# Storing the recurrence's normaliser vectors as rows transposed on chip

## The chip, the cores and the metric

The kernel runs on one core of a Trainium2 chip. Its time is the device time of one execution in microseconds (us); the kernel before has a median of 781.07 us over three runs (779.24 to 781.85). One further execution was profiled, and every row below is from it: it took 777.49 us, of which the span from the first to the last instruction is 775.7 us.

## The reference

One step of a layer with three head groups over a shared input projection: differential attention (A), a matrix-memory recurrence (B, mLSTM) and cross-attention into a memory (M), for a prompt of 1024 tokens and, beside it, for 8 decoding streams of 16 tokens with a cache of 1024. Group B is what matters here. For each of its 4 heads of dimension 64 it carries a matrix C and a vector n, the normaliser, from chunk to chunk:

```python
C = decay[..., None, None] * C0 + jnp.einsum('bhs,bhsd,bhse->bhde', wS, k, v)
n = decay[..., None] * n0 + jnp.einsum('bhs,bhsd->bhd', wS, k)
```

The final states are outputs of the kernel: `p_C` (4 heads x 64 x 64) and `p_n` (4 x 64) for the prompt, `s_C` (8 streams x 4 x 64 x 64) and `s_n` (8 x 4 x 64) for the decoding streams. All are 4-byte floats in device memory.

## The kernel before, in words

Nine row tiles of 128 tokens are worked on: tiles 0 to 7 are the prompt, tile 8 (`DEC`) holds the 8 x 16 decoding tokens. Phases follow each other (A0 to A3, G, M, B0, B1, O0, O1): each loads and splits a block of weights and projects all nine tiles through it (three passes of high and low parts, `project`, matmuls of L97 into the PSUM banks `ps_z` and `ps_y`). What is done with a projected tile is a generator in stages, and a pipe advances those of earlier tiles while later tiles are projected (`feed`). Attention of the decoding streams (`dec_attention`, with key and value loads `kc`, `vc` of 512 KB each) is woven in through phases M, B0 and B1.

Phases B0 and B1 (`pr` 0 and 1) do two heads each. `b_stages` is the work on one tile: `mlstm_in` (L1012) copies and transposes q and k, `mlstm_scores` (L1038) loads rows of `mtd` broadcast over the partitions into `mb` (L1042) and makes the decay mask from them on POOL (L1043) and ACT (L1045), then come the products and the new state. For the prompt the state of a pair of heads is one tile `csn` of 128 x 130: partition (head, d), columns 0 to 63 of a head's 65 being C and the 65th being n. After the last prompt tile (L1149) four stores are issued for the pair, C and n of each head. For the decoding streams (`mlstm_decode`, L1077) the state is the tile `C0`, 128 partitions (head, d) by 8 streams by 65 columns. It has one buffer (`bufs=1`): the load for pair 1 (L1079) can be issued only when everything that reads pair 0's tile is done, the two stores at L1111 and L1112 among it. In B0 the decoding tile goes first, in B1 third.

In both cases n is spread over the partitions, one 4-byte element (per stream) in each, and it is stored from there: 1024 elements for one pair's `s_n` (L1112), 64 for one head's `p_n` (L1152).

All loads and stores are issued by SyncE (SP) from one in-order list. The order of the instructions of every engine is worked out by a scheduler from its own model of durations, with the priorities that the code sets (`ahead`); within an engine that order is then fixed, and an instruction that waits holds up all behind it. PSUM tiles with the tag `tp`, into which all transposes write, have two buffers.

Of the kernel before, what the change touches and what calls it, by code (L numbers as in the profile page):

```python
# [11 lines left out]
F32 = mybir.dt.float32  # L12
# [8 lines left out]
P = 128  # L21
# [3 lines left out]
NPT = 8  # L25
# [35 lines left out]
def hymba_step(ctx: ExitStack, tc: tile.TileContext, a: dict, o: dict):  # L61
    nc = tc.nc
    V, S, G, PE, SY = nc.vector, nc.scalar, nc.gpsimd, nc.tensor, nc.sync

    def pool(name, side="left"):
        return tc.tile_pool(name=name, bufs=1, side=side, reuse_waits="tile")
# [5 lines left out]
    def bank(tag):  # L72
        bufs = {"z": 2, "y": 1, "tp": 2, "s": 2, "av": 1}[tag]
        return ps.tile([P, 512], F32, tag=tag, name=f"ps_{tag}", bufs=bufs)
# [3 lines left out]
    def copy(e, out, in_):  # L78
        if e == "S":
            S.copy(out, in_)  # L80
        else:
            ENG[e].tensor_copy(out, in_)
# [13 lines left out]
    def mm(out, lhsT, rhs, start=True, stop=True):  # L96
        PE.matmul(out, lhsT, rhs, start=start, stop=stop)  # L97
# [11 lines left out]
    def bc(ap, n):  # L109

        return ap.unsqueeze(len(ap.shape)).broadcast_to(list(ap.shape) + [n])

    def rep(ap, n):

        return ap.unsqueeze(1).broadcast_to([ap.shape[0], n] + list(ap.shape[1:]))

    def heads(ap, h):
        return ap.rearrange("p (h e) -> p h e", h=h)

    def flat(ap):  # L120
        return ap.rearrange("p a b -> p (a b)")


    ident = cpool.tile([P, P], F32, name="ident")
# [887 lines left out]
    def mlstm_in(bw, nb, bufs, t, pr, z):  # L1012

        hs = slice(2 * pr, 2 * pr + 2)
        vx, qn, cs = bufs
        qp, qn = qn, bw.tile([P, 2, 64], F32, tag="bqn", name="bqn", bufs=nb)
        S.copy(flat(qn), z[:, 0:128])
        kg = bw.tile([P, 2, 64], F32, tag="kg", name="kg", bufs=nb)
        S.activation(flat(kg), z[:, 128:256], AF.Copy, scale=0.125)
        kw = bw.tile([P, 2, 64], F32, tag="kw", name="kw", bufs=nb)  # L1020
        G.tensor_tensor(kw, kg, bc(wsN[:, t, hs], 64), ALU.mult)
        S.copy(vx[:, :, 0:64], heads(z[:, 256:384], 2))
        gt = bw.tile([P, P], F32, tag="bgt", name="bgt", bufs=nb)
        SY.dma_start(out=gt, in_=gated[t][:, 512 + pr * P:512 + (pr + 1) * P])
        th = bw.tile([P, P], F32, tag="bth", name="bth", bufs=2)
        S.activation(th, z[:, 384:512], AF.Tanh, scale=0.5)
        V.scalar_tensor_tensor(gt, th, 1.0, gt, ALU.add, ALU.mult)
        tp = bank("tp").rearrange("p (a b) -> p a b", a=4)
        PE.transpose(tp[:, 0], flat(kg), ident)
        PE.transpose(tp[:, 1], flat(qn), ident)  # L1030
        qk = bw.tile([P, 2, P], F32, tag="qk", name="qk", bufs=nb)
        V.tensor_copy(qk, tp[:, 0:2])
        for i in range(2):
            sl = slice(i * 64, i * 64 + 64)
            copy("VS"[i], qp[sl, i * P:(i + 1) * P], tp[sl, 1])
        return qk, kw, gt

    def mlstm_scores(bw, nb, t, pr, mask, qk, qp):  # L1038

        mb = bw.tile([P, 2, P], F32, tag="mb", name="mb", bufs=nb)  # L1040
        r0 = t * 4 + 2 * pr
        SY.dma_start(out=flat(mb), in_=mtd[r0:r0 + 2, :].rearrange("h t -> (h t)").partition_broadcast(P))  # L1042
        G.tensor_tensor(mb, rep(mask, 2), mb, ALU.subtract)  # L1043
        for h2 in range(2):
            S.activation(mb[:, h2], mb[:, h2], AF.Exp, bias=aN[:, t, 2 * pr + h2:2 * pr + h2 + 1])  # L1045
        st = bank("s")[:, 0:256]
        mm(st, qk[:, 0], qp)
        V.tensor_tensor(flat(mb), st, flat(mb), ALU.mult)
        return mb

    def mlstm_out(bw, nb, t, pr, nm, carried, dst, gate):
# [22 lines left out]
            )  # L1074
        SY.dma_start(out=dst, in_=flat(hb))

    def mlstm_decode(pr, z, bufs):  # L1077
        C0 = bw.tile([P, 8, 65], F32, tag="C0", name="C0", bufs=1)
        SY.dma_start(out=C0, in_=a["Cn"][pr])  # L1079
        qk, kw, gt = mlstm_in(bw, nb, bufs, DEC, pr, z)  # L1080
        yield
        at = mlstm_scores(bw, nb, DEC, pr, maskd, qk, bufs[1])
        yield
        vx = bufs[0]
        for i in range(2):
            V.tensor_copy(
                gqz.rearrange("p (c i) x -> p c i x", i=2)[:, :, i, i * 16:i * 16 + 16],
                qk[:, 1].rearrange("p (c i q) -> p c i q", i=2, q=16)[:, :, i],
            )
        nmf = bank("s")  # L1090
        nm, carried = heads(nmf[:, 0:130], 2), heads(nmf[:, 130:260], 2)
        for i in range(2):
            for h2 in range(2):
                sl = slice(h2 * 64, h2 * 64 + 64)
                copy("VG"[h2], csd[sl, :, h2 * 65:h2 * 65 + 65], C0[sl, i::2])
            for c in range(4):
                mm(nmf[c * 32:c * 32 + 32, 130:260], gqz[:, 2 * c + i, :], csd[:, c, :], i == 0, i == 1)
        for h2 in range(2):
            mm(nm[:, h2], at[:, h2], vx[:, h2])
        mlstm_out(bw, nb, DEC, pr, nm, carried, mixd[DEC][:, 512 + pr * P:640 + pr * P], gt)  # L1100
        V.tensor_tensor(C0, C0, bc(dec[:, DEC, pr], 65), ALU.mult)
        for c in range(0, NB, 4):
            km = bw.tile([P, 4, P], F32, tag="km", name="km", bufs=2)
            (G, V)[c // 4].tensor_tensor(km, rep(flat(kw), 4), bc(bm[:, c:c + 4], P), ALU.mult)
            up = heads(bank("s")[:, 0:260], 4)
            for j in range(4):
                for h2 in range(2):
                    mm(up[h2 * 64:h2 * 64 + 64, j], km[:, j, h2 * 64:h2 * 64 + 64], vx[:, h2])
            V.tensor_tensor(C0[:, c:c + 4], up, C0[:, c:c + 4], ALU.add)
        hs = slice(2 * pr, 2 * pr + 2)  # L1110
        SY.dma_start(out=o["s_C"][0, :, hs].rearrange("b h d e -> (h d) b e"), in_=C0[:, :, 0:64])  # L1111
        SY.dma_start(  # L1112
            out=o["s_n"][0, :, hs].rearrange("b h (d o) -> (h d) b o", o=1), in_=C0[:, :, 64:65]
        )

    cst = {}

    def b_stages(pr, t, i_):
        def run(z):
            if t == DEC:  # L1120
                yield from mlstm_decode(pr, z, bufs2[i_ % nb])
                return
            bufs = bufs2[i_ % nb]
            vx, qn, csn = bufs
            qk, kw, gt = mlstm_in(bw, nb, bufs, t, pr, z)
            yield
            at = mlstm_scores(bw, nb, t, pr, maskp, qk, qn)
            yield
            nmf = bank("s")
            nm, carried = heads(nmf[:, 0:130], 2), None  # L1130
            cs = cst.get(pr)
            if t:
                carried = heads(nmf[:, 130:260], 2)
                mm(flat(carried), qk[:, 1], cs)
            for h2 in range(2):
                mm(nm[:, h2], at[:, h2], vx[:, h2])


            up = nmf[:, 260:390]
            mm(up, flat(kw), flat(vx))  # L1140
            for h2 in range(2):
                sl, cc = slice(h2 * 64, h2 * 64 + 64), slice(h2 * 65, h2 * 65 + 65)
                if t == 0:
                    V.tensor_copy(csn[sl, cc], up[sl, cc])
                else:
                    V.scalar_tensor_tensor(
                        csn[sl, cc], cs[sl, cc], dec[sl, t, pr, 0:1], up[sl, cc], ALU.mult, ALU.add
                    )
                if t == NPT - 1:  # L1149
                    h = 2 * pr + h2  # L1150
                    SY.dma_start(out=o["p_C"][0, 0, h], in_=csn[sl, h2 * 65:h2 * 65 + 64])
                    SY.dma_start(  # L1152
                        out=o["p_n"][0, 0, h].rearrange("(d o) -> d o", o=1),
                        in_=csn[sl, h2 * 65 + 64:h2 * 65 + 65],
                    )
            cst[pr] = csn
            mlstm_out(bw, nb, t, pr, nm, carried, mixd[t][:, 512 + pr * P:512 + (pr + 1) * P], gt)

        return run
# [65 lines left out]
    bw = ctx.enter_context(pool("bwork", "right"))  # L1225
# [121 lines left out]
```

## Time and profile before

| what | value |
|---|---|
| median of three runs | 781.07 us (779.24 to 781.85) |
| the profiled execution, and its span | 777.49 us, 775.7 us |
| busy: TensorE (PE), VectorE (DVE), ScalarE (ACT), GpSimd (POOL) | 730.5, 471.8, 333.3, 237.1 us |
| mean granted TensorE clock | 0.982 of full speed |
| DMA queues, share of 16 engines over the span | 43.1% |
| chain that ended last: PE, DVE, DMA | 77%, 8%, 7% |

PE is the matmul row and PEld its weight loads. A granted clock of 1.00 is TensorE's upper level (2.4 GHz), 0.50 the lower (1.2 GHz). Times of events are microseconds from the span's start. In a timeline row, the bracket at the end tells how long the engine had been idle and whose end it waited for. The name `C` in the trace is the tile `C0`, `cs` the tile `csn`.

### The profile page before, as it was taken

To read this page: it belongs to the slowest core of one execution; us is meant where nothing else is said; L and a number is where in the kernel's file an instruction comes from. 1 tells how busy PE (TensorE), PEld (TensorE's weight loads), DVE (VectorE), ACT (ScalarE), POOL (GpSimd) and SP (SyncE) were. 2 spreads that over 40 slices of the span, in tenths; PEclk is the share of its full clock that TensorE was granted. 3 is DMA by queue.
4 is the path that set the end of the run, shared out by engine and by line. 5 is a ranking of instruction groups with operands and counts; after the bars stand their busy time and mean duration, and the time that the engine had idled before them with its cause. 6 is when DMAs were issued, how large, how long until landed. Compare 5 with 4: busy or idle time off the path is not lost.

```text
span 775.7 us, 14506 instructions
## 1 busy us (share of the span) xinstructions
PE 730.5 (94%) x4944; PEld 603.6 (78%) x4944; DVE 471.8 (61%) x1460; ACT 333.3 (43%) x978; POOL 237.1 (31%) x336
## 2 busy tenths in 40 slices
PE   7998899999999999999999899699999948999998
PEld 6776688878888888998878677467777737778887
DVE  6888786677788778678685844136833535842011
ACT  6666635574564466465354452224422323411200
POOL 6653451232133222336311413102211215521500
PEclk9999999999999999999999999889999979999999
DMA  8733430151014112415401529358978316984332
GB/s 314 278 110 94 148 99 28 34 160 49 19 51 124 49 28 63 120 55 144 152 15 18 188 73 336 95 183 301 327 222 248 120 41 222 310 208 136 109 108 95
DMA packets 84388, 106.20 MB, mean 137 GB/s; under 512 B 16054, under 2 KB 52698, under 8 KB 84314
## 3 DMA queue, kind: packets, MB, share of 16 engines
q1 hardware_dynamic: 84314, 105.28, 43.1%
q8 instruction: 39, 0.64, 0.4%
q14 instruction: 35, 0.29, 0.1%
HBM read 86.01 MB, written 19.23 MB: 136 GB/s over the span
## 4 chain that ended last, share of the span: by engine, by line
PE 77%; DVE 8%; DMA 7%; issue 3%; POOL 2%; ACT 2%; SPq 0%; DVEq 0%; POOLq 0%; ACTq 0%
PE ps_z L97 40%; PE ps_y L97 16%; PE ps_s L97 8%; PE ps_av L97 6%; DMA mb<-mtd 3%; DMA wraw<-in_w_in_dram 2%; PE ps_tp L461 2%; DMA out_dram<-C 1%; DVE wl L240 1%; PE ps_tp L202 1%; PE ps_tp L406 1%; PE ps_tp L902 1%; DVE xT L296 1%; POOL asm L135 1%; DMA mxt<-in_mem_prompt_dram 1%
## 5 line engine op out<-in xcount | busy, mean ns | idle before, releaser
L97 PE MATMUL ps_z<-wh,htl 128*128 128x512 f32 (+2 forms) x552 | 212.7, 387 | 0.0
L97 PE MATMUL ps_z<-wh,hth 128*128 128x512 f32 (+2 forms) x552 | 199.2, 393 | 3.9 <-ACT hth L282 2.6
L97 PE MATMUL ps_z<-wl,hth 128*128 128x512 f32 (+2 forms) x552 | 184.1, 387 | 0.0
L97 PEld LDWEIGHTS ps_z<-wh,hth 128*128 128x128 f32 x552 | 103.0, 189 | 25.2 <-ACT hth L282 2.8
L97 PEld LDWEIGHTS ps_z<-wh,htl 128*128 128x128 f32 x552 | 104.2, 189 | 18.2 <-DVE htl L283 0.4
L97 PEld LDWEIGHTS ps_z<-wl,hth 128*128 128x128 f32 x552 | 103.1, 189 | 18.5 <-issue 0.8
L97 PE MATMUL ps_y<-wh,htl 128*128 128x512 f32 (+2 forms) x176 | 66.5, 380 | 0.0
L97 PE MATMUL ps_y<-wh,hth 128*128 128x512 f32 (+2 forms) x176 | 64.3, 386 | 0.0
L135 POOL TENSOR_TENSOR asm<-asm,nhalf 128x4 f32<-128x4 f32 x36 | 39.6, 1100 | 75.0 <-DVE asm L139 59.7
L445 ACT ACTIVATE usx<-usx,usm 128x1024 f32<-128x1024 f32 (+7 forms) x64 | 49.7, 778 | 29.1 <-DVE usm L439 26.8
L97 PE MATMUL ps_y<-wl,hth 128*128 128x512 f32 (+2 forms) x176 | 60.4, 376 | 0.1
L240 DVE SCALAR_TENSOR_TENSOR wl<-wraw,gnm,wh 128x512 fp32r<-128x512 f32 (+1 forms) x62 | 47.3, 785 | 4.2 <-ACT wh L233 4.0
L233 ACT ACTIVATE wh<-wraw,gnm 128x512 fp32r<-128x512 f32 (+1 forms) x56 | 38.1, 707 | 20.6 <-DMA wraw<-in_w_in_dram 18.5
L97 PE MATMUL ps_s<-aqk 128*128 128x256 f32 (+1 forms) x160 | 42.0, 288 | 2.2 <-ACT aqk L414 2.2
L439 DVE CUSTOM_DVE_ANT_0 usx<-ps_s,tab 128x512 f32<-128x512 f32 (+3 forms) x64 | 37.0, 587 | 9.0 <-PE ps_s L97 7.6
L135 POOL TENSOR_TENSOR usm<-usm,nhalf 128x1 f32<-128x1 f32 x32 | 19.6, 612 | 72.9 <-DVE usm L469 68.4
L97 PE MATMUL ps_s<-akl,aqk 128*128 128x256 f32 (+1 forms) x160 | 41.0, 283 | 0.0
L97 PE MATMUL ps_av<-avg,wth 128*128 128x128 f32 x288 | 38.7, 276 | 0.2 <-DVE uot L471 0.2
L97 PEld LDWEIGHTS ps_av<-avg,wth 128*128 128x128 f32 x288 | 36.9, 191 | 2.5 <-ACT wth L462 0.6
L97 PEld LDWEIGHTS ps_y<-wh,hth 128*128 128x128 f32 x176 | 33.8, 193 | 5.7
L97 PEld LDWEIGHTS ps_y<-wh,htl 128*128 128x128 f32 x176 | 33.9, 193 | 5.3
L97 PEld LDWEIGHTS ps_y<-wl,hth 128*128 128x128 f32 x176 | 33.0, 188 | 5.7 <-DVE wl L240 0.5
(448 smaller groups left out, 1379.6 us busy)
## 6 DMA issues: line engine op xcount, KB each, us to landing
kc<-in_kT_dram SPq DMA_DIRECT2D x32, 512.0 KB, 6.5
vc<-in_cache_attn_v_dram SPq DMA_DIRECT2D x32, 512.0 KB, 7.0
wraw<-in_w_in_dram SPq DMA_DIRECT2D x56, 256.0 KB, 3.1
omx<-mixd SPq DMA_DIRECT2D x9, 512.0 KB, 6.4
out_dram<-oxt SPq DMA_DIRECT2D x17, 256.0 KB, 2.1
xt<-in_x_prompt_dram SPq DMA_DIRECT2D x8, 512.0 KB, 7.5
wraw<-in_w_out_dram SPq DMA_DIRECT2D x16, 256.0 KB, 4.1
oxt<-in_x_prompt_dram SPq DMA_DIRECT2D x16, 256.0 KB, 3.6
```

Of the source, the lines that this page charges most:

```text
L97: PE.matmul(out, lhsT, rhs, start=start, stop=stop)
L135: G.tensor_tensor(dst, ss, nhalf[:, 0:ss.shape[1]], ALU.pow)
L202: PE.transpose(tv[:, i, :], src[:, (c + i) * P:(c + i + 1) * P], ident)
L233: S.activation(wh[:, 0:n], raw[:, 0:n], AF.Copy, scale=g_)
L240: V.scalar_tensor_tensor(wl[:, 0:n], raw[:, 0:n], g_, f(wh[:, 0:n]), ALU.mult, ALU.subtract)
L296: V.scalar_tensor_tensor(xT[:, cs], xT[:, cs], math.sqrt(D), rep(rb, 4), ALU.mult, ALU.mult)
L406: PE.transpose(tp[:, i], flat(nd[:, 2 * i:2 * i + 2]), ident)
L439: V.tensor_tensor_reduce(s_[:, c * 512:c * 512 + w], sp[:, 0:w], tab[:, tx:tx + w], -slope, BIG if c == 0 else sm[:, m:m + 1], ALU.add, AL ...
L445: S.activation(s_[:, 0:nk], s_[:, 0:nk], AF.Exp, bias=last, scale=-1.0, accum_out=sm[:, 4 + m:5 + m])
L461: PE.transpose(tp[:, i], sx[0][:, (c + i) * P:(c + i + 1) * P], ident)
L902: PE.transpose(tp[0:pn, c - c0, :], se[:, c * P:c * P + pn], ident)
```

## The change

A helper `store_n` takes the columns that hold n, transposes them on TensorE into a PSUM tile (n rows of 128), copies that to an SBUF tile `nt` on ScalarE, and stores rows. For `s_n` the store at L1112 becomes one store of 8 rows of 128 elements (512 bytes each, both heads of a pair for one stream). For `p_n` the two stores of a pair at L1152 become two stores of one row of 64 elements each (256 bytes), taken from the diagonal blocks of a 2 x 128 tile, issued after both heads are updated. The stores of C stay as they are.

```diff
+    def store_n(dst, cols, diag=False):
+
+        n = cols.shape[1]
+        tp = bank("tp")
+        PE.transpose(tp[0:n, 0:P], cols, ident)
+        nt = bw.tile([8, P], F32, tag="nt", name="nt", bufs=1)
+        S.copy(nt[0:n], tp[0:n, 0:P])
+        if diag:
+            for h2 in range(2):
+                SY.dma_start(out=dst[h2:h2 + 1], in_=nt[h2:h2 + 1, h2 * 64:h2 * 64 + 64])
+        else:
+            SY.dma_start(out=dst, in_=nt[0:n])
+
     def mlstm_decode(pr, z, bufs):
...
         SY.dma_start(out=o["s_C"][0, :, hs].rearrange("b h d e -> (h d) b e"), in_=C0[:, :, 0:64])
-        SY.dma_start(
-            out=o["s_n"][0, :, hs].rearrange("b h (d o) -> (h d) b o", o=1), in_=C0[:, :, 64:65]
-        )
+        store_n(o["s_n"][0, :, hs].rearrange("b h d -> b (h d)"), C0[:, :, 64])
...
                     SY.dma_start(out=o["p_C"][0, 0, h], in_=csn[sl, h2 * 65:h2 * 65 + 64])
-                    SY.dma_start(
-                        out=o["p_n"][0, 0, h].rearrange("(d o) -> d o", o=1),
-                        in_=csn[sl, h2 * 65 + 64:h2 * 65 + 65],
-                    )
+            if t == NPT - 1:
+                hs = slice(2 * pr, 2 * pr + 2)
+                store_n(o["p_n"][0, 0, hs], csn[:, 64::65], True)
```

## Rows read from the trace of the kernel before

**Rows 1.** The page's busy times: engine, busy us, share, instructions.
```profile
PE 730.5 (94%) x4944; PEld 603.6 (78%) x4944; DVE 471.8 (61%) x1460; ACT 333.3 (43%) x978; POOL 237.1 (31%) x336
```

**Rows 2.** Chain that ended last, 484 to 512 us: start, us, what.
```profile
485.87 11.63 DMA out_dram<-C
497.56 3.33 DMA C<-in_Cn_dram
...
500.92 0.29 DVE csd L82
...
504.45 0.29 DVE ewt L82
...
505.44 1.96 PE ps_av L97 x16
...
508.01 3.15 PE ps_z L97 x9
```

**Rows 3.** Timeline of PE, 494 to 506 us: start, us, instruction, idle before.
```profile
494.88 1.96 PE L97 MATMUL ps_y<-vc,ewt 128*32 128x128 f32 x64
504.78 0.66 PE L97 MATMUL ps_y<-vn,ewt 128*32 128x128 f32 x8 [7.94 <-DVE ewt L82]
```

**Rows 4.** Windows: stretch, length, PE PEld DVE ACT POOL busy, PEclk, DMA, GB/s.
```profile
490.00:492.00 2.00, 2.00 (x13) 1.56 (x12) 0.07 (x1) 0.40 (x1) 0.00 (x0) 1.00 0.00 0
...
500.00:502.00 2.00, 0.00 (x0) 0.00 (x0) 0.65 (x3) 0.30 (x2) 0.46 (x1) 0.50 0.71 188
...
626.00:628.00 2.00, 0.00 (x0) 0.00 (x0) 0.00 (x0) 0.00 (x0) 0.00 (x0) 1.00 0.05 4
...
630.00:632.00 2.00, 0.00 (x0) 0.00 (x0) 0.00 (x0) 0.00 (x0) 0.00 (x0) 0.50 0.01 3
```

**Rows 5.** Timeline of SP, 484 to 488 us.
```profile
485.43 0.39 SPq L1111 DMA_DIRECT2D out_dram<-C  x1
```

**Rows 6.** Line L1111 by itself: issue to landing of the store of C.
```profile
DMA to landing us min/median/max: 2.7/2.9/3.1
```

**Rows 7.** Chain that ended last, 600 to 650 us.
```profile
621.70 13.30 DMA mb<-mtd
...
636.78 1.22 PE ps_y L97 x4
638.00 1.20 PE ps_s L97 x2
639.20 7.45 PE ps_y L97 x24
```

**Rows 8.** Timeline of PE, 624 to 640 us.
```profile
636.78 1.22 PE L97 MATMUL ps_y<-ems,sr 128*128 128x128 f32 x4 [10.97 <-ACT ems L914]
```

**Rows 9.** Tile mb: issue to landing of its 18 loads.
```profile
DMA to landing us min/median/max: 3.0/5.0/13.3
```

**Rows 10.** Chain that ended last, 560 to 600 us.
```profile
565.93 2.28 PE ps_z L97 x9
...
576.08 6.77 DMA mb<-mtd
...
588.33 1.02 PE ps_av L97 x16
...
590.22 0.45 PE ps_y L97 x4
590.66 0.43 PE ps_s L97 x2
...
591.70 5.46 PE ps_y L97 x24
```

**Rows 11.** Timeline of PE, 584 to 592 us.
```profile
585.58 0.28 PE L902 MATMUL ps_tp<-ident,se 128*16 128x128 f32 x1 [1.25 <-DVE ewt L82]
```

**Rows 12.** Timeline of ACT, 588 to 590 us.
```profile
589.07 0.26 ACT L80 COPY qn<-ps_tp 64x128 f32<-64x128 f32 x1 [0.78 <-DVE qn L82]
```

**Rows 13.** Waits: who waited for whom, us in total, times, longest.
```profile
ACT mb L1045 <- POOL mb L1043: 43.6, 13, 11.4
```

## The prediction

> **What bounds the kernel now.** I read the page first: PE is busy for 94% of the span [rows 1], so a stall elsewhere counts only where it opens a hole in PE. Then I read the chain of waits in order of time and looked for pieces that are no PE work. Most are short. The long ones in the last 300 us are three DMA pieces, and each lies beside one of the stores of n. For each I took the PE timeline (is PE idle, and who ends it?) and the windows (what do the DMA engines do meanwhile?).
>
> Hole 1, pair 0's decoding state. The store of C is issued at 485.43 [rows 5], that of n at 485.87; the chain then waits 11.63 us for a store out of C0, reloads C0 for 3.33 us, and DVE's copy `csd`, which needs it, starts at 500.92 [rows 2]. DVE is in order, and the small copy `ewt` queued behind it starts at 504.45 [rows 2]. PE had ended its work at 494.88 + 1.96 = 496.84 and idles 7.94 us for that copy [rows 3]. During the wait the DMA engines show a share of 0.00 and 0 GB/s [rows 4]: nothing else is being moved. The clock is at its lower level in 500:502, after PE had stopped [rows 4].
>
> Hole 2, pair 1's decoding state. A load of `mb` issued at 621.70, just behind that pair's stores, takes 13.30 us [rows 7], where the median load of `mb` takes 5.0 and the fastest 3.0 [rows 9]. PE idles 10.97 us, from 625.81 to 636.78 [rows 8]; the DMA share is 0.05 and 0.01 in that time and the clock falls again [rows 4].
>
> Hole 3, pair 0's prompt state. A load of `mb` at 576.08, with the four stores of C and n issued right after it, takes 6.77 us [rows 10], and PE idles 1.25 us [rows 11]. Pair 1's prompt stores have no such wait in the chain: PE has projections queued there, and I cost that end at nothing.
>
> **The change, part by part.** What goes is 2 x 1024 + 4 x 64 = 2304 stored elements of 4 bytes; what comes is 2 stores of 8 rows and 4 of one row. The number of issues on SP stays the same, six.
>
> Hole 1: the reload of C0 now waits for the store of C and for a transpose that reads C0. The store of C lands 2.7 to 3.1 us after its issue [rows 6], with 2.9 at 488.3. The reload takes its 3.33 to 491.7, some 9.2 us before 500.92, and the copy `ewt`, 3.53 + 0.29 behind `csd` [rows 2], ends at about 495.5. That is before PE is through at 496.84, so the whole 7.94 goes. What is late next is PE itself; 1.3 us of slack is left. Next is the clock: 16 `ps_av` matmuls took 1.96 at the lower level against 1.02 later, 9 of `ps_z` took 3.15 against 2.28 [rows 2, 10]; 0.94 + 0.87 = 1.81 returns if PE doesn't stop. Together 9.75.
>
> Hole 2: with `mb` landing L after 621.70, PE can go on at 621.70 + L + 1.78, where 1.78 is the way from landing (635.00) to PE (636.78) today [rows 7, 8]. L = 3.0 gives 626.48, L = 5.0 gives 628.48; the hole shrinks to 0.67 or 2.67. I take the median, so 10.97 - 2.67 = 8.30. The clock term: 4 `ps_y` 1.22 against 0.45, 2 `ps_s` 1.20 against 0.43, 24 `ps_y` 7.45 against 5.46 [rows 7, 10], together 3.53. Sum 11.83.
>
> Hole 3: with 3.0 to 5.0 instead of 6.77, everything behind comes 1.8 to 3.8 us earlier, more than the 1.25 that PE waited. Gain 1.25.
>
> Added: four transposes with 128 streamed columns from 2 or 8 stationary ones. The nearest row is the transpose from 16 columns, 0.28 [rows 11]. Each may make PE wait for DVE to finish the state, or for one of the two `tp` buffers; the trace has no such wait, so its bounds are nothing (the scheduler finds a place where the data is there) and 1.25, the wait of that same row. I take 0.35, nearer to the lower end since small waits are the rule in the chain: 4 x 0.63 = 2.5, bounds 1.1 and 6.1. The four copies on ACT, some 0.26 each [rows 12], cost nothing: ACT is busy 43% [rows 1]; without that cover they add 1.0. The tile `nt` has one buffer, but its four uses are 40 us and more apart. On SP a store of `nt` waits for its copy on ACT, and behind it stand the reload of C0, the next `vc`, `kc` and `mb`; at hole 1 the reload waits until 488.3 anyway, and at hole 2 `mb` goes out 1.4 us behind the stores, about what a transpose and a copy need.
>
> Sum: 9.75 + 11.83 + 1.25 - 2.5 = 20.3 us. The profiled execution took 777.49, which gives 757.2; it was 3.6 below the median of the runs, and against that median it is 781.07 - 20.3 = 760.8. I predict 761. Its own range: L between 3.0 and 5.0 gives up to 2.0 more, cheap transposes 1.4 more and dear ones 3.6 less; the scheduler orders everything behind 485 us anew, for which I allow 4 us both ways. That is 753 to 768.
>
> In the Trainium skill, "DMA: Bandwidth & Descriptors", section "Specifications", gives 512 bytes as the least transfer for full rate and says that the engines do a read-modify-write below it. That speaks against this change: the stores of C have rows of 256 bytes and stay. If these rows cost what the 4-byte ones do, no hole would close; the trace bears it out badly, since the store of C landed in 2.7 to 3.1 us [rows 6]. This is the second rival below.
>
> **The rivals.**
> First, one of the two large holes stays. For it: a chain of in-order engines stands behind each, and the scheduler may put another waiting instruction in front of `ewt` or `ems`. Against it: both holes are ended by one DMA piece [rows 2, 7], and at hole 1 there are 1.3 us of slack. Price 9.75 or 11.83: 781.07 - 20.3 + 9.75 = 770.5, or 772.6.
>
> Second, the change leaves the cause where it is: the waits belong to the stores of C, 1024 rows of 256 bytes for a pair, or to the traffic before them. For it: at hole 1 the chain's name fits either store out of C0 and a landing of the store of n isn't shown. Against it: the landing of the store of C [rows 6] and idle DMA engines at 490:492 [rows 4], with only the n store outstanding. Then nothing is gained and 2.5 is paid: 783.6, slower.
>
> Third, the slower side: one store becomes a chain over PE, ACT and SP, all in order. Its place is the copy on ACT: where the scheduler puts it behind an exponential that waits for its mask (ACT did so 13 times, 43.6 us in all, mean 3.4, longest 11.4 [rows 13]), the store of `nt` is late, and SP holds back every load behind it. Four places at 3.4 cost 13.6, which leaves 774.4; with the longest at both decoding places and the mean at the others it is 29.6, and 781.07 - 20.3 + 29.6 = 790.4. It decides from an average of 5.1 us per place. Against it: ACT has idle time, and the copy needs no load.
>
> **How the numbers follow.** Forecast 0.66; one hole stays 0.20; the C stores are to blame 0.05; the ACT chain strong enough to be slower 0.05, weaker (about 774) 0.04. A difference of 0.3% is 2.3 us. Slower is 0.05 of the second rival less a little, and 0.05 of the third: 0.09. Within 0.3%: 0.04, from cases where two of these meet. Faster: 0.87. The range that should hold 8 in 10 takes the forecast's own low end, one microsecond lower since other loads near 680 us also pass the n stores, and at the upper end the case of one hole staying and the weak ACT chain: 752 to 774.
>
> **What would show it right or wrong.** Right: behind the store of C the reload of C0 is issued about 3 us later, not 11.6; no PE idle stretch over 3 us near 485 to 505 nor behind pair 1's decoding state; no window with the clock at 0.50 in these stretches; `mb` at most about 8 us at the longest. The new transposes should be four `ps_tp` matmuls from C and cs, at about 0.28. Wrong: `mb` loads still at 13 us or the reload at 11 us with no 4-byte stores left would show the second rival; a PE hole ended by DVE or ACT with DMA early, the first; SP idle at a store from `nt`, released by ACT, for several us, the third.

## The result, and the profile after

The changed kernel takes 757.47 us (median of four runs, 754.36 to 759.58) against 780.15 (four, 778.17 to 781.85): a ratio of 0.9707, with a 95% interval of 0.9661 to 0.9752, or 22.7 us less. 761 was predicted, with 752 to 774 as the range. The profiled execution of after took 754.36 us, its span is 752.6.

The same instructions can be looked up in the chain of waits of both kernels, and their times give an account of where the 23.1 us between the two spans came from:

| instruction on PE | before | after | difference |
|---|---|---|---|
| `ps_y` x72, ahead of hole 1 | 494.88 | 492.59 | -2.29 |
| `ps_z` x16, behind hole 1 | 514.71 | 501.65 | -13.06 |
| `ps_y` x24, ahead of hole 3 | 568.21 | 555.46 | -12.75 |
| `ps_y` x24, ahead of hole 2 | 611.24 | 597.41 | -13.83 |
| `ps_s` x8, behind hole 2 | 646.66 | 622.06 | -24.60 |
| end of the span | 775.7 | 752.6 | -23.1 |

The first 2.29 us lie ahead of everything that the change touches: one execution against another. Hole 1 gave 10.77 us (-13.06 less -2.29), hole 3 about 1.1, hole 2 10.77; 0.3 went again between holes 1 and 3, and 1.5 behind hole 2. Without the first line 20.8 us are left, where the prediction's sum was 20.3.

The windows of the two stretches (columns as in [rows 4]) part each of the large gains into idle time and slower matmuls. Hole 1, before and after, then hole 2, before and after:

```profile
494.88:514.71 19.83, 11.89 (x126) 8.65 (x126) 4.70 (x20) 3.66 (x15) 2.24 (x4) 0.74 0.67 223
492.59:501.65 9.06, 9.06 (x126) 7.43 (x127) 2.89 (x11) 2.70 (x9) 0.67 (x1) 1.00 0.86 298
...
611.24:646.66 35.42, 24.07 (x198) 19.50 (x198) 11.99 (x49) 8.35 (x31) 6.00 (x9) 0.81 0.22 58
597.41:622.06 24.65, 21.51 (x200) 17.30 (x199) 11.40 (x49) 8.59 (x32) 6.01 (x9) 1.00 0.25 73
```

At hole 1 PE's idle time falls from 7.94 us to nothing and its busy time by 2.83. At hole 2 the idle time falls by 8.21 (from 11.35 to 3.14) and the busy time by 2.56. A new transpose is in each of the busy times of after, 0.21 and 0.11 us by the chain; the granted clock of both stretches is 1.00 now.

The busy line of the page of after (engine, busy us, share, instructions), to set against [rows 1]: PE has 4 instructions more and 4.9 us less busy time; behind 460 us none of it runs at the lower clock any more.

```profile
PE 725.6 (96%) x4948; PEld 599.2 (80%) x4948; DVE 472.5 (63%) x1460; ACT 334.2 (44%) x982; POOL 237.1 (32%) x336
```

The chain that ended last, of after, around hole 1 (start, us, what), against [rows 2]:

```profile
492.59 2.10 PE ps_y L97 x72
494.69 0.90 PE ps_av L97 x16
495.59 0.21 PE ps_tp L1081
495.80 0.11 PE ps_tp L1029
...
501.65 3.67 PE ps_z L97 x16
```

Where the chain of before left PE for a store, a reload and two copies on DVE, this one stays on PE. The new transpose (L1081) takes 0.21 us of it. The windows of after (as in [rows 4]) show why there is no clock term: PE is busy for all of both stretches and the clock stays at 1.00, and in the first the DMA engines move 263 GB/s where they moved nothing.

```profile
490.00:492.00 2.00, 2.00 (x10) 1.65 (x10) 1.11 (x6) 0.79 (x5) 1.10 (x2) 1.00 0.75 263
500.00:502.00 2.00, 2.00 (x18) 1.48 (x17) 0.67 (x3) 0.86 (x1) 0.00 (x0) 1.00 1.05 381
```

The timeline of SP, after, 482 to 500 us (the issue of each DMA), does not show what the prediction had expected:

```profile
483.04 0.39 SPq L1124 DMA_DIRECT2D out_dram<-C  x1
...
497.83 0.39 SPq L1088 DMA_DIRECT2D out_dram<-nt  x1
498.40 0.33 SPq L1092 DMA_DIRECT2D C<-in_Cn_dram  x1
```

The reload of C0 goes out 15.4 us behind the store of C, later than before, where it was 12.1 (497.56 less 485.43 [rows 2, 5]). The scheduler has written a new order: transpose, copy and store of n come 12 to 15 us behind the store of C, the reload behind them, and DVE's copy `csd` (505.75 now) no longer stands ahead of `ewt`.

Hole 2, after: the chain, and PE's timeline in its place (the bracket: idle before, and who ended it). The load of `mb` takes 2.86 us instead of 13.30 [rows 7]; of the 10.97 us of idle PE [rows 8] two waits are left, 1.24 us for a `tp` buffer that the copy to `nt` had not yet read, and 1.74 us for `qn`, which stands behind a load of `bgt`.

```profile
607.20 2.86 DMA mb<-mtd
...
610.93 3.33 DMA bgt<-gated
```

```profile
608.63 1.09 PE L902 MATMUL ps_tp<-ident,se 128*128 128x128 f32 x8 [1.24 <-ACT nt L1083]
615.89 0.70 PE L97 MATMUL ps_s<-qn,qk 128*128 128x256 f32 x2 [1.74 <-ACT qn L80]
```

The first of the two comes from ACT. The transpose that the copy to `nt` waits for is done at 606.05 (605.78 and 0.27), but on ACT two exponentials stand ahead of the copy, and they wait for their mask from POOL (ACT's timeline, after):

```profile
607.74 0.69 ACT L1045 ACTIVATE mb<-mb,nat 128x128 f32<-128x128 f32 x2 [1.70 <-POOL mb L1043]
608.34 0.24 ACT L1083 COPY nt<-ps_tp 8x128 f32<-8x128 f32 x1
```

The wait is passed on: PE's transposes of `se` start at 608.63, DVE's copy `ewt` of them runs until 610.01, and `hb` follows at 610.05. The chain names the landing of `mb` there (610.06), which comes 0.05 us behind the end of `ewt`, though `hb` is made of `bns`, `bsm` and `bgt`.

The landing of `mb` in after, to set against [rows 9]:

```profile
DMA to landing us min/median/max: 3.1/3.3/6.9
```

What was added: two lines each of the views of L1081 (the transpose) and L1083 (the copy) in after, durations in ns as min/median/max. They agree with [rows 11, 12].

```profile
L1081 PE MATMUL ps_tp<-ident,C x2: 272/274/277, 495.5 to 605.8; 128*8 128x128 f32 x2
L1081 PE MATMUL ps_tp<-ident,cs x2: 271/272/273, 574.0 to 654.2; 128*2 128x128 f32 x2
```

```profile
L1083 ACT COPY nt<-ps_tp x4: 238/252/255, 495.8 to 654.7; 8x128 f32<-8x128 f32 x2, 2x128 f32<-2x128 f32 x2
```

### The profile page after: what moved, and what is told of

Read it like the earlier page. It is cut to its first block, busy times and chain, and to the rows that moved or that the text cites. A ratio compares the mean times of both kernels' runs of the same rounds, so it can differ in the third digit from the quotient of the medians.

```text
span 752.6 us, 14527 instructions
## 1 busy us (share of the span) xinstructions
PE 725.6 (96%) x4948; PEld 599.2 (80%) x4948; DVE 472.5 (63%) x1460; ACT 334.2 (44%) x982; POOL 237.1 (32%) x336
## 4 chain that ended last, share of the span: by engine, by line
PE 79%; DVE 10%; DMA 5%; issue 3%; POOL 2%; ACT 2%; DVEq 0%; SPq 0%; POOLq 0%; ACTq 0%
PE ps_z L97 42%; PE ps_y L97 15%; PE ps_s L97 8%; PE ps_av L97 6%; DMA wraw<-in_w_in_dram 2%; PE ps_tp L461 2%; DVE wl L240 2%; PE ps_tp L202 1%; DMA bgt<-gated 1%; PE ps_tp L406 1%; PE ps_tp L902 1%; PE ps_tp L645 1%; DVE xT L296 1%; POOL asm L135 1%; DMA mxt<-in_mem_prompt_dram 1%
```

## The experiments

**No n at all.** The result leaves two readings: that the stores were slow, or that the new order did it. The first run takes the stores away and leaves the old order.

```diff
-        SY.dma_start(out=o["s_n"][0, :, hs].rearrange(...), in_=C0[:, :, 64:65])
...
-                    SY.dma_start(out=o["p_n"][0, 0, h].rearrange(...), in_=csn[...])
```

> The kernel before without its stores of n (s_n and p_n are not written; nothing else is left out). The order of PE, DVE, ACT and POOL stays that of the kernel before, the stores of C stay. Theory T (while 4-byte elements are being written, whatever stands behind them on the DMA queues and whoever waits for their landing is held): all three holes close at the old order, the reload of C0 is issued about 3 us behind the store of C, the longest load of mb is 8 us or less, and the time is 753 to 758, some 22 to 25 us below the kernel before. Theory O (the gain comes from the order that the scheduler found for the new kernel, in which the reload of C0 and the copy csd come later): hole 1 stays, because csd still stands ahead of ewt, and 8 to 11 us of the gain are missing: about 766 to 770. Theory C (the stores of C, rows of 256 bytes, cause the waits): nothing changes, 778 to 782.

Measured: 756.11 us (752.95 to 758.92), ratio 0.967 (0.9632 to 0.9708). Both holes go with the order as it was, and here the prediction's path is seen. SP's timeline of this kernel:

```profile
486.19 0.64 SPq L1111 DMA_DIRECT2D out_dram<-C  x1
489.04 0.33 SPq L1079 DMA_DIRECT2D C<-in_Cn_dram  x1
```

The reload is issued 2.85 us behind the store of C, which has landed by then, and what stayed of holes 2 and 1 (waits of PE in this kernel: us in total, times, longest) is 1.3 and 1.1 us:

```profile
PE ps_y L97 <- ACT ems L914: 1.3, 1, 1.3
PE ps_y L97 <- DVE ewt L82: 1.1, 1, 1.1
```

The stores of C are still there, and the holes are gone: they are not what held PE. This run also tells what the new stores and transposes cost beside none at all, in another order: 1.4 us by the medians (757.47 less 756.11), 2.9 by the ratios, and the intervals don't tell either from nothing.

**The new order with 4-byte elements.** The counterpart: the changed kernel, order and transposes as they are, but `nt` is stored as every second element, so that each element is a piece of 4 bytes again.

```diff
...
-            SY.dma_start(out=dst, in_=nt[0:n])
+            for j in range(2):
+                SY.dma_start(out=dst[:, j::2].unsqueeze(2), in_=nt[0:n, j::2].unsqueeze(2))
```

> The changed kernel with one thing undone: the tile nt is still made by transpose and copy and stored from there, but the stores take every second element (two stores instead of one), so that each element is again 4 bytes. The order of the four compute engines is that of the changed kernel. Theory T: the stores of n hold the queue again; the loads behind them (bgt at hole 2, kc, vc and the reload of C0 at hole 1) land late, and at least the hole behind pair 1's decoding state is back: 765 to 780. Theory O: the order decides and the sizes don't: 755 to 760, as the changed kernel.

Measured: 790.53 us (789.4 to 793.24), ratio 1.0114 (1.0077 to 1.0152): slower than before, outside both expectations. The new order alone gives nothing; with it 4-byte elements cost even more. The chain and PE's waits of this kernel show holes of the old kind at new places:

```profile
503.79 14.55 DMA C<-in_Cn_dram
...
593.55 10.44 DMA mb<-mtd
...
630.32 10.20 DMA bgt<-gated
```

```profile
PE ps_s L97 <- ACT qn L80: 8.6, 1, 8.6
PE ps_tp L902 <- DVE ewt L82: 6.5, 1, 6.5
PE ps_y L97 <- DMA mvc<-in_cache_mem_v_dram: 5.6, 3, 3.7
```

Why it is more than before (a store cut differently over 8 partitions, six more issues on SP, or a place just ahead of urgent loads) was not separated.

**The same elements, far apart.** Is it their size, or their neighbourhood? This kernel is the one before, with as many 4-byte elements going to a scratch buffer in device memory, each to 512 bytes of its own.

```diff
-            out=o["s_n"][0, :, hs].rearrange("b h (d o) -> (h d) b o", o=1), in_=C0[:, :, 64:65]
+            out=spr[pr, 0:1024].rearrange("(p b) e -> p b e", b=8)[:, :, 0:1], in_=C0[:, :, 64:65]
...
```

> The kernel before, with the 4-byte elements of n stored to a scratch array in which each element has 512 bytes of its own (s_n and p_n themselves are not written). Count, size, place of issue and the order of all engines are those of the kernel before; only the neighbourhood of the elements in device memory changes. Theory T in its plain form (the size of an element alone decides): the three holes stay, 777 to 783. Theory N (elements are slow because many of them fall side by side into the same few hundred bytes and are written by several DMA engines at once): the holes close, 753 to 760.

Measured: 757.14 us (755.55 to 759.41), ratio 0.9687 (0.9657 to 0.9716). Nothing is transposed, as many elements of the same size are stored, and the gain is all there. In SP's timeline the reload follows 3.9 us behind the store of the elements, in PE's waits holes 1 and 2 are 0.4 and 2.4 us:

```profile
487.24 0.58 SPq L1113 DMA_DIRECT2D spr<-C  x1
491.17 0.33 SPq L1080 DMA_DIRECT2D C<-in_Cn_dram  x1
```

```profile
PE ps_y L97 <- ACT ems L915: 2.4, 1, 2.4
PE ps_y L97 <- DVE ewt L82: 0.4, 1, 0.4
```

So my theory that 4-byte pieces as such are slow fell. What is slow is many of them into the same short stretches of memory, or else any such store into an output of the kernel instead of a scratch buffer: this run changed both, and the next ones part them.

**Kinds of stores by themselves.** Two small kernels compute nothing of the layer: they issue one store, right behind it a load of 128 KB, and DVE waits for the load; three times for each kind. In the first, stores of one kind could start before those of another had landed:

> A kernel of its own that leaves out the whole computation: eleven kinds of store, each three times, each followed by one broadcast load of 128 KB on the same queue; VectorE waits for the load, then for the store. It measures how long a store and the load behind it take with nothing else on the chip: none (32 bytes), 1024 elements of 4 bytes as s_n has them, the same with 64 or 512 bytes of own space for each, the same packed into 4 KB, 1024 elements of 64 and of 256 bytes, 64 elements of 4 bytes as p_n has them, the same with 512 bytes of own space, 64 of 256 bytes, and 8 x 2 rows of 256 bytes. Theory T (size): all 4-byte kinds of 1024 elements hold the load for 9 us and more, those of 64 elements for 3 us and more, those of 64 bytes and up less than 2 us over the empty case. Theory N (neighbours): only the kinds whose elements share lines (s_n, packed, p_n) are slow; with own space they cost less than 2 us over the empty case.

It settles nothing: the kind with an empty store (one row of 32 bytes) already waited up to 21 us among the others' traffic.

The second makes each store wait for the load before it:

```diff
+        V.tensor_scalar(flat(st), ones, acc[:, 0:1], None, ALU.add)
+        for r in range(3):
+            V.tensor_scalar(flat(st), flat(st), acc[:, 0:1], None, ALU.add)
+            V.tensor_copy(pb[:, 0:8], flat(st)[:, 0:8])
+            SY.dma_start(out=dst, in_=src(st))
+            SY.dma_start(out=pb, in_=a["x_prompt"][0, r, 0:256].partition_broadcast(P))
+            V.tensor_copy(acc, pb[:, 0:8])
...
```

> The stores by themselves again, now with every store written and waited for before the next begins (in e4 the stores of later kinds had started at once and overlapped). The computation is left out. Per kind: time from a store's issue to the landing of the 128 KB load issued behind it, and to its own landing. Theory N (elements that share a few hundred bytes with others being written by other DMA engines are slow; size alone is not): sn and the same layout in a scratch array (snscr) hold the load for 9 us or more and pn for 3 us or more over the empty case, both alike; 1024 elements of 4 bytes with 64 or 512 bytes of own space, in scratch or in an output (ownout), stay within 2 us of the empty case, as do 64 and 256 byte elements and pnown; packed, where each engine writes a stretch of 256 bytes of its own, tells whether sharing between engines or sharing at all counts. Rival X (the scratch array is fast and the output slow, whatever the neighbourhood): sn slow, snscr fast, ownout slow.

DVE's timeline, one of three rows for each kind; the bracket is the time from the start of the two until the load has landed. The kinds shown are: the empty store; `s_n` as before; the same layout in scratch; 1024 elements side by side; 1024 with 16, 64 and 512 bytes of their own; 1024 pieces of 256 bytes; `p_n` as before (64 elements); the same with 512 bytes each; 16 rows of 256 bytes.

```profile
10.81 0.17 DVE L82 COPY acc<-pb_none 128x8 f32<-128x8 f32 x1 [3.10 <-DMA pb_none<-in_x_prompt_dram]
...
33.87 0.17 DVE L82 COPY acc<-pb_sn 128x8 f32<-128x8 f32 x1 [15.91 <-DMA pb_sn<-in_x_prompt_dram]
...
115.81 0.17 DVE L82 COPY acc<-pb_snscr 128x8 f32<-128x8 f32 x1 [13.82 <-DMA pb_snscr<-in_x_prompt_dram]
...
147.26 0.17 DVE L82 COPY acc<-pb_packed 128x8 f32<-128x8 f32 x1 [8.80 <-DMA pb_packed<-in_x_prompt_dram]
...
156.31 0.17 DVE L82 COPY acc<-pb_own_xvi 128x8 f32<-128x8 f32 x1 [6.90 <-DMA pb_own_xvi<-in_x_prompt_dram]
...
180.73 0.17 DVE L82 COPY acc<-pb_own_lxiv 128x8 f32<-128x8 f32 x1 [5.57 <-DMA pb_own_lxiv<-in_x_prompt_dram]
...
208.81 0.17 DVE L82 COPY acc<-pb_own_dxii 128x8 f32<-128x8 f32 x1 [5.22 <-DMA pb_own_dxii<-in_x_prompt_dram]
...
263.67 0.17 DVE L82 COPY acc<-pb_wide_cclvi 128x8 f32<-128x8 f32 x1 [5.12 <-DMA pb_wide_cclvi<-in_x_prompt_dram]
...
302.53 0.17 DVE L82 COPY acc<-pb_pn 128x8 f32<-128x8 f32 x1 [6.76 <-DMA pb_pn<-in_x_prompt_dram]
...
319.41 0.17 DVE L82 COPY acc<-pb_pnown 128x8 f32<-128x8 f32 x1 [3.94 <-DMA pb_pnown<-in_x_prompt_dram]
...
324.76 0.17 DVE L82 COPY acc<-pb_rows 128x8 f32<-128x8 f32 x1 [3.19 <-DMA pb_rows<-in_x_prompt_dram]
```

Each kind's mean of three, less the 3.27 us of the empty store, is what the store costs the load behind it: `s_n` 12.6 us, its layout in scratch 10.6, 16 rows of 256 bytes, near to the 8 rows of 512 that replace it, nothing (3.23 us). Between them the cost falls with distance: 5.4 us side by side, 3.5 with 16 bytes each, 2.3 with 64, 1.8 with 512. The same number of pieces of 256 bytes costs 1.6, so what is left at 512 goes with the number of pieces, not with their size. Two kinds that are not shown fit: 1024 elements in an output of the kernel, each with 4 KB of its own, cost 1.9, and 1024 pieces of 64 bytes 1.5. So an output as such is not slow, and a scratch buffer as such not fast. The 64 elements of one `p_n` cost 3.7, and 0.6 apart.

**The two halves.** First each half of the change by itself, in whatever order the scheduler then writes; the diffs are the two halves of the one shown.

> The change for s_n alone; p_n is stored as before, two 64-element stores of 4 bytes for each pair. The account by holes: holes 1 and 2 close, hole 3 (1.25 us) stays and the transposes of p_n are saved: 757 to 760, about 21 us below the kernel before. Rival (the p_n stores hold more than hole 3 shows, through the loads of vc, kc and omx behind them): 762 and more.

> The change for p_n alone; s_n is stored as before. The account by holes: holes 1 and 2 stay, hole 3 closes: 777 to 780, 1 to 2 us below the kernel before or not told apart from it. Rival (p_n holds more): 775 and less.

Measured: `s_n` alone 762.06 us (759.79 to 766.87), ratio 0.9779 (0.9733 to 0.9824); `p_n` alone 776.54 (774.79 to 777.98), ratio 0.9945 (0.9924 to 0.9966), that is 4.3 us less (2.7 to 5.9). The first is just at the bound of the rival, the second between the two expectations: both lean to `p_n` holding more than hole 3. Then the same by leaving out, with the old order on the four compute engines:

```diff
-                    SY.dma_start(out=o["p_n"][0, 0, h].rearrange(...), in_=csn[...])
```

> The kernel before without the four stores of p_n (that output is left out); the order of the instructions on PE, DVE, ACT and POOL is that of before. Theory H (the stores of p_n hold up more than hole 3: each takes 8.0 to 9.9 us to land, and the vc, mb and omx loads queued behind crawl): ratio to before 0.992 to 0.997, that is 775 to 778.5 us, PE hole 3 gone, holes 1 and 2 unchanged at 8 and 11 us. Rival S (p_n is worth its hole of 1.25 us and no more; the 4 us of the earlier run came from the new order): ratio 0.998 to 1.000, 779 to 781 us.

```diff
-        SY.dma_start(out=o["s_n"][0, :, hs].rearrange(...), in_=C0[:, :, 64:65])
```

> The kernel before without the two stores of s_n (that output is left out); order of the four compute engines as before. If the parts add up, it and the one without p_n together give the 24.9 us that taking away both gave: theory H expects 759 to 762 us (20 to 22 us gained), holes 1 and 2 gone and hole 3 still there; rival S expects 756 to 758 us (23 to 25 us gained). If the sum of the two gains is above 27 or below 22 us, they overlap or hide each other.

Measured: without `p_n` 776.78 us, ratio 0.9927 (0.9902 to 0.9952), 3.8 to 7.7 us less; without `s_n` 760.25, ratio 0.972 (0.9692 to 0.9748), 19.7 to 24.1 less. The times are those of theory H: `p_n` is worth more than hole 3. By the ratios the two gains are 5.7 and 21.9 us and add up to 27.6, against 25.8 for both at once (3.3% of 781). That is a little above the 27 that had been set as the sign that they overlap; the intervals allow a plain sum too.

The profile without `s_n` shows a part of what `p_n` holds, at pair 0. Here the load of `mb` lands early (issued at 565.99, POOL starts on it at 569.11), but a load of `bgt`, issued 3 us behind the last store of `p_n` (568.50), takes 12.10 us and the `mb` behind it 8.30. The chain, and PE's wait at its end:

```profile
571.46 12.10 DMA bgt<-gated
...
583.64 8.30 DMA mb<-mtd
```

```profile
595.98 1.33 PE L902 MATMUL ps_tp<-ident,se 128*128 128x128 f32 x5 [2.57 <-ACT qn L80]
```

With another 0.95 us of waits for `mvc` at pair 1 (676 to 677 us) that is 3.5 us, of the 4.1 by which its median lies above that of the kernel without any n (760.25 less 756.11).

Pair 1, which the prediction costed at nothing, shows these stores too. The windows (columns as in [rows 4]) are of before and of the kernel without `p_n`, at the same place of the work, which that profile reaches 3.4 us later (its `ps_z` x10 starts at 681.81, before at 678.37): with the stores the DMA engines are the busier (0.96 against 0.78) and move 95 GB/s instead of 238.

```profile
680.00:685.00 5.00, 5.00 (x40) 3.84 (x39) 3.10 (x8) 0.95 (x3) 1.67 (x3) 1.00 0.96 95
```

```profile
683.40:688.40 5.00, 5.00 (x39) 3.83 (x39) 3.10 (x9) 0.99 (x3) 1.71 (x3) 1.00 0.78 238
```

But PE is busy for all of it in both. And the profiled execution without `p_n` took 781.15 us, the longest of its six: of the gain in the medians its trace shows no more than hole 3, 1.4 us (`ps_y` x24 to `ps_y` x24 around it: 572.45 to 614.06, against 568.21 to 611.24). So two more executions of the unchanged kernel were profiled.

> The kernel before once more, for a second profiled execution: the first one took 777.49 us, 3.5 below the median of its runs, so the gain of 4 to 6 us that leaving out the stores of p_n gives may lie in what the first did not show. Theory H: an execution near the median shows its extra 2 to 5 us behind the stores of p_n, as a hole 3 of 3 to 5 us near 585 us or a PE wait near 675 to 700. Rival V: what it has more lies ahead of 480 us, in phases that come before every store of n, and the stretch from the last ps_y of pair 0's decoding state to the end is as long as in the first profile, within 1 us.

> The kernel before a third time, for a third profiled execution, with the same two expectations as the second: theory H puts what it has more than 777.49 us behind the stores of p_n, rival V ahead of 480 us.

They took 780.37 and 779.18 us, 2.9 and 1.7 more than the first. In the second profile PE does wait behind those stores (its timeline, 690 to 700 us):

```profile
697.90 0.43 PE L97 MATMUL ps_y<-mvc,mwt 128*32 128x64 f32 x16 [1.13 <-DMA mvc<-in_cache_mem_v_dram]
698.51 0.43 PE L97 MATMUL ps_y<-mvc,mwt 128*32 128x64 f32 x16 [0.18 <-DMA mvc<-in_cache_mem_v_dram]
```

That is 1.3 of its 2.9 us; another 1.0 lies ahead of 480 us (`ps_av` x16 at 478.05 against 477.06). In the third profile that wait isn't there and 1.5 of the 1.7 us lie ahead of 480 (478.59). Hole 3 was 1.25, 1.39 and 0.85 us in the three. Waits for `mvc` at pair 1 are otherwise seen only in profiles of kernels that store `p_n` in 4-byte elements side by side or nearly so (0.95 us without `s_n`, 5.6 in the new order with 4-byte elements), and not in all of them; those without such stores have none. So H is shown in part: 0.85 to 1.4 us of hole 3, and 1.3 at pair 1 in one of three profiles. The rest of the 3.8 to 7.7 us stays open.

**One more buffer.** Since the reload of C0 is late in the new order, a second buffer for it:

```diff
-        C0 = bw.tile([P, 8, 65], F32, tag="C0", name="C0", bufs=1)
+        C0 = bw.tile([P, 8, 65], F32, tag="C0", name="C0", bufs=2)
```

> The changed kernel with two buffers for C0, so that the reload for pair 1 waits for nothing. In the changed kernel the reload is issued at 498.4 behind the store of nt and takes 7.3 us to land, and DVE waits 2.7 us for it in the copy csd. If that wait is on the path, 2 to 3 us are gained: 753 to 755 against 757.5. If it lies beside PE work, as the chain of the changed kernel says (PE has no hole there), nothing is gained: 756 to 759.

Measured: 757.24 us (755.7 to 759.75), ratio to before 0.9706 (0.9672 to 0.9741), the same as the change without it (0.9707). The late reload lies beside PE's work and costs nothing that these runs can tell.

## Why the prediction was right, and which steps of it were not

**Hole 1** was sized 9.75 and gave 10.77. The 7.94 us of idle time went whole, as sized. The clock term was put at 1.81 and came to 2.83, or 3.04 without the new transpose in it: it had been added up from two groups of matmuls, and others ran at the lower clock too, `ps_y` x72 for one (1.96 and 0.66 us [rows 3], 2.10 now). And the step that led there, "behind the store of C the reload of C0 is issued about 3 us later", with `csd` and so `ewt` early, is not what happened: it is issued 15.4 us behind, and `csd` has moved out of `ewt`'s way. The step does hold in the old order: the run without n has it at 2.85 us. I allowed "4 us both ways" for the new order without asking which instructions it could part; here it parted just the two that stood one behind the other. That the hole closed by this other way as well was luck.

**Hole 2** was sized 11.83 and gave 10.77. `mb` landed in 2.86 us, faster than the median that I took, but two waits of 1.24 and 1.74 us remain, together 2.98 against the 2.67 that I had left over; with the small ones beside them PE's idle time fell by 8.21, for 8.30. The mis-sized term is the clock's, 3.53: PE's busy time fell by 2.56, or 2.67 without the new transpose. Its largest part came as worked out, the same `ps_y` x24 takes 5.46 us (616.59 to 622.06 in the chain of after), the figure that I had put against 7.45; but the two `ps_s`, which stand behind the new wait, take 0.70 where I had put 0.43.

**Hole 3** gave 1.1 for 1.25. The load of `mb` that waited there had been issued 1.1 us ahead of the first store of `p_n` (576.08 against 577.22 in SP's timeline) and took 6.77 us; without these stores it takes at most 3.4 in the same order (issued at 580.32, POOL starts on it at 583.66). So they also held a load that was already under way; in the kernel without `s_n` this load landed early, and they held the next one, of `bgt`. The mis-sized term is beside it, pair 1's prompt stores: "PE has projections queued there, and I cost that end at nothing". Together with hole 3 these stores are worth 3.8 to 7.7 us, by the runs that leave `p_n` out. That PE is covered there was read from one execution, which took 3.6 us less than the median; in another PE waits 1.3 us in that place.

**The four transposes** were put at 2.5. In the chain they take 0.11 to 0.21 each, and one wait of 1.24 us for a `tp` buffer comes from them: some 1.9. It was a wait for the buffers that I had named, at the upper bound that I had given it, once of four times; only it is another transpose that waits, for the copy to `nt`.

Of the signs that had been named, all but the early reload came: no wait of PE over 1.74 us in these stretches, the clock at 1.00, `mb` at 6.9 us at the longest, four transposes at 0.27.

**The rivals.** One hole stays: no. The stores of C to blame: no. They are still issued in the run without n, where the holes are gone, and 1024 pieces of 256 bytes by themselves cost 1.6 us. The Trainium skill's rule in "DMA: Bandwidth & Descriptors", section "Specifications" (a read-modify-write below 512 bytes), speaks of size; here 4 bytes apart cost what 256 bytes do, and 4 bytes among neighbours seven times that, so the measurement decides for the neighbourhood. Whether a read-modify-write is what the neighbours wait for, no run shows. The chain over ACT: in part, and not as a chain to the store. Once of four times the copy did stand behind an exponential that waits for its mask (2.3 us, 606.05 to 608.34), as this rival said. But the store of `nt` goes out behind `mb` (608.60 against 607.20) and holds no load that the chain shows; the price was the `tp` buffer, 1.24 us on PE.

**The sum** was right by 0.5 us in the traces (20.3 against 20.8) and by 2.4 in the medians (20.3 against 22.7). So close a sum is luck in part: hole 1 gave 1.0 more and hole 2 1.1 less than forecast, by two clock terms that were wrong in opposite ways, and the 2.5 taken off for the transposes, whose cost of some 1.9 lies mostly inside the holes' gains, came near to the 1.8 that went in other stretches. In the medians, what `p_n` gives beyond hole 3 may be a part of the 2.4; no run shows it.

## What to carry to other kernels

In the window of a hole, look at the DMA share and the GB/s together: a queue that is open and moves nothing, or is busy and moves little, points to the stores issued near the load that the chain names. Before storing a column that is spread over the partitions, turn it: a transpose and a copy of 0.27 and 0.25 us replaced a store that held the load behind it for 12.6 us. And where one part is costed at nothing because PE has work, see in a second execution whether it still has.

## What the runs showed of the hardware that was not expected

A store of 1024 elements of 4 bytes costs the load behind it anything from 1.8 us, with 512 bytes for each element, to 12.6, in the order of `s_n`, in which neighbouring partitions write neighbouring elements; with 64 elements it is 0.6 or 3.7. Output or scratch matters less (in the order of `s_n` waits of 15.3 to 16.3 us against 12.9 to 14.9). And executions of one kernel differ by 1.0 to 1.5 us before they come to the changed place, as much as many a term of the sum.
